# Four column groups for the left sums, one result partition, and two stores at the end of a column-sum kernel

## Chip, cores, metric

One core of one Trainium2 chip. The metric is device time in microseconds (us), the median of several executions. I also use the trace: the time from the landing of the last input byte to the end of the span, "the tail" below, is not disturbed by what the 620 us before it do. Landings, and the last increments of the stores (the steps by which a DMA counts up its semaphore as it completes), are read from the semaphore records of the trace; everything else from the profile.

## The reference

```python
def setup_inputs():
    batch, seq, dim = 32, 1024, 2048
    return {"grad_output": np.random.randn(batch, seq, dim).astype(np.float32)}

def reference(grad_output):
    return np.sum(grad_output, axis=(0, 1)).astype(np.float32)
```

32,768 rows of 2048 columns, 268 MB, are summed to one row.

## The kernel before

Rows stream in through one DMA queue into a ring in SBUF; VectorE adds them together. The last rows are instead summed over the 128 partitions by TensorE (a matmul with a column of ones), accumulating in PSUM. The very last rows come in a left part (1536 columns) and a right part (512), so that the left part can be finished while the right one still lands.

```python
LEFT = ((0, 512, 0), (512, 512, 1), (1024, 512, 2))      # first column, columns, column group
RIGHT = ((1536, 256, 2), (1792, 256, 3))
...
    for bank, pieces in enumerate((LEFT, RIGHT)):
        for lo, n, g in pieces:
            sums[lo] = psum[32 * g : 32 * g + 1, 512 * bank : 512 * bank + n]
...
    with nc.tensor.Fori(0, ROUNDS):
        for j, lane in enumerate(row_in):
            take(nc.tensor, lane)
            ... # one filler matmul of 256 columns into group 3
            matmuls(j * D, LEFT + RIGHT).then_inc(used, 1)
    matmuls(at * D, LEFT + RIGHT, wait=(step, n_step))
    for x, lo, pieces, lane, stop in final:
        then = (mm_left if pieces is LEFT else mm_right) if stop else None
        matmuls(x, pieces, lo, wait=(lane, 16), then=then)
...
    res = ring[:, res_at : res_at + 512]
    nc.scalar.copy(out=res[:96, :], in_=psum[:96, :512])._wait_ge(mm_left, len(LEFT)).then_inc(left, 1)
    half = res[96:97, :].rearrange("p (h n) -> p h n", h=2)
    nc.vector.tensor_copy(out=half[:, 0, :], in_=sums[RIGHT[0][0]])._wait_ge(mm_right, 1).then_inc(right_0, 1)
    nc.scalar.copy(out=half[:, 1, :], in_=sums[RIGHT[1][0]])._wait_ge(mm_right, 2).then_inc(right_1, 1)
    nc.sync.wait_ge(left, 1)
    nc.sync.wait_ge(right_0, 1)
    nc.sync.dma_start(out=out.rearrange("(g n) -> g n", g=4), in_=res[0:128:32, :])._wait_ge(right_1, 1).then_inc(done, 16)
```

The result lies in four rows, on partitions 0, 32, 64 and 96, and leaves in one store of four descriptors.

## Time and profile before

| | before |
|---|---|
| time, median of 3 | 629.28 us |
| span of the profiled run | 627.5 us |
| last input byte lands | 623.25 us |
| store's issue | 624.46 to 625.11 us |
| store's last increment | 626.22 us |
| tail (last input byte to end) | 4.30 us |

The span is filled by the input stream, at 428 GB/s. A line of the timeline reads: start, duration, engine, line, operation, output and input with shapes, count, and in brackets how long the engine sat idle and what ended it. SPq is the queue that issues the DMAs; the duration there is what the issue holds the queue, not the transfer.

### The profile page before, as it was taken

The numbers are of one execution on the slowest core, as the hardware profiler recorded it, in microseconds if no ns is written. First come the engines' busy times: TensorE is split into PE (matmuls) and PEld (weight loads), VectorE is DVE, ScalarE is ACT, GpSimd is POOL, SyncE is SP. The second block draws the span as 40 slices with busy tenths as digits, with TensorE's granted clock in tenths as the row PEclk, the third lists the DMA queues.
The fourth block names the chain that finished last, engine by engine and source line by source line (L and its number), as shares of the span: only waits on it lengthen the run. The fifth ranks groups of instructions, "written<-read, shape, count | busy, mean of one in ns | idle before, by whom it ended". The sixth has DMA issues, their size and how long they took to land. (4 is left out here: it accounts for less than half of the span.)

```text
span 627.5 us, 575 instructions
## 1 busy us (share of the span) xinstructions
PE 18.2 (3%) x136; PEld 4.9 (1%) x136; DVE 532.3 (85%) x68; ACT 2.4 (0%) x4; POOL 0.3 (0%) x5
## 2 busy tenths in 40 slices
PE   0000000000000000000000000000000000000055
PEld 0000000000000000000000000000000000000011
DVE  0349988889888898888988889988889888898994
ACT  0000000000000000000000000000000000000000
POOL 0000000000000000000000000000000000000000
PEclk9999999999999999999999999999999999999999
DMA  9999999999999999999999999999999999999996
GB/s 401 401 468 401 468 401 468 401 468 401 468 401 468 401 468 401 468 401 468 401 464 405 455 414 447 422 439 430 426 443 426 443 414 455 405 464 401 442 416 279
DMA packets 5912, 268.45 MB, mean 428 GB/s; under 512 B 660, under 2 KB 660, under 8 KB 1176
## 3 DMA queue, kind: packets, MB, share of 16 engines
q1 hardware_dynamic: 5912, 268.45, 99.1%
HBM read 268.44 MB, written 0.01 MB: 428 GB/s over the span
## 5 line engine op out<-in xcount | busy, mean ns | idle before, releaser
L118 DVE TENSOR_TENSOR ring<-ring 128x8192 f32<-128x8192 f32 (+2 forms) x65 | 528.6, 8134 | 84.9 <-DVEq L112 82.1
L183 PE MATMUL psum<-ring,ones 128*1 128x512 f32 (+1 forms) x120 | 18.2, 560 | 598.6 <-DMA ring<-in_grad_output_dram 598.5
L183 PEld LDWEIGHTS psum<-ring,ones 128*1 128x1 f32 x120 | 4.3, 86 | 608.4 <-DMA ring<-in_grad_output_dram 600.5
L200 PE MATMUL psum<-ring,ones 128*1 128x256 f32 x16 | 5.3, 412 | 7.0 <-PEq L112 7.0
L215 DVE COPY ring<-psum 1x256 f32<-1x256 f32 x1 | 0.4, 424 | 5.9 <-PE psum L183 5.9
L213 ACT COPY ring<-psum 96x512 f32<-96x512 f32 x1 | 0.6, 582 | 620.8 <-PE psum L183 620.8
L118 DVE TENSOR_TENSOR ring<-ring,head 128x2048 f32<-128x2048 f32 x1 | 2.3, 2292 | 0.1
L131 DVE MEMSET psum<- 128x1024 f32 x1 | 0.9, 912 | 1.2 <-SPq L121 1.2
L200 PEld LDWEIGHTS psum<-ring,ones 128*1 128x1 f32 x16 | 1.3, 92 | 10.0 <-issue 9.8
L211 ACT ACT_TABLE_LOAD x1 | 1.3, 1283 | 0.9 <-SPq L121 0.9
L216 ACT COPY ring<-psum 1x256 f32<-1x256 f32 x1 | 0.4, 365 | 0.3 <-PE psum L183 0.3
L211 ACT COPY warm<-ones 1x1 f32<-1x1 f32 x1 | 0.2, 190 | 0.0
L238 POOL MEMSET const-bfloat16-1.0<- 128x1 bf16 x1 | 0.1, 102 | 0.0
L238 POOL MEMSET const-uint8-127<- 128x1 uint8 x1 | 0.1, 102 | 0.0
L125 POOL MEMSET ones<- 128x1 f32 x1 | 0.1, 99 | 0.5 <-SPq L121 0.5
L238 POOL MEMSET const-float32-0.0<- 128x1 f32 x1 | 0.1, 99 | 0.2 <-issue 0.2
L238 POOL MEMSET const-float32-1.0<- 128x1 f32 x1 | 0.1, 99 | 0.0
## 6 DMA issues: line engine op xcount, KB each, us to landing
ring<-in_grad_output_dram SPq DMA_DIRECT2D x1, 5120.0 KB, 22.6
ring<-in_grad_output_dram SPq DMA_DIRECT2D x1, 4096.0 KB, 14.7
ring<-in_grad_output_dram SPq DMA_DIRECT2D x4, 1024.0 KB, 9.5
ring<-in_grad_output_dram SPq DMA_DIRECT2D x2, 768.0 KB, 13.5
head<-in_grad_output_dram SPq DMA_DIRECT2D x1, 1024.0 KB, 4.8
ring<-in_grad_output_dram SPq DMA_DIRECT2D x2, 256.0 KB, 14.5
ring<-in_grad_output_dram SPq DMA_DIRECT2D x30, 29.8
out_dram<-ring SPq DMA_DIRECT2D x1, 8.0 KB
```

The source lines that it names most:

```text
L118: return nc.vector.tensor_add(out=rows(at, n), in0=rows(at, n), in1=other)
L125: nc.gpsimd.memset(ones[:], 1.0).then_inc(one, 1)
L131: nc.vector.memset(psum[:, : 2 * 512], 0.0).then_inc(zero, 1)
L183: mat = nc.tensor.matmul(sums[lo], lhsT=ones[:], rhs=ring[:, x : x + n], start=start, stop=then is not None)
L200: nc.tensor.matmul(psum[96:97, 2 * 512 : 2 * 512 + FILLER], lhsT=ones[:], rhs=rows(j, 1)[:, :FILLER], start=True, stop=True)
L211: nc.scalar.copy(out=warm[:], in_=ones[0:1, :])._wait_ge(one, 1)
L213: nc.scalar.copy(out=res[:96, :], in_=psum[:96, :512])._wait_ge(mm_left, len(LEFT)).then_inc(left, 1)
L215: nc.vector.tensor_copy(out=half[:, 0, :], in_=sums[RIGHT[0][0]])._wait_ge(mm_right, 1).then_inc(right_0, 1)
L216: nc.scalar.copy(out=half[:, 1, :], in_=sums[RIGHT[1][0]])._wait_ge(mm_right, 2).then_inc(right_1, 1)
L238: nc = _bacc.Bacc("TRN2", target_bir_lowering=False, num_devices=1)
```

## The change

The intent: get the left sums out of the way early and in parallel, bring all sums to one partition, and let each part leave in a store of one descriptor.

```diff
-LEFT = ((0, 512, 0), (512, 512, 1), (1024, 512, 2))
+LEFT = ((0, 416, 0), (416, 416, 1), (832, 352, 2), (1184, 352, 3))
 RIGHT = ((1536, 256, 2), (1792, 256, 3))
 ...
-    res = ring[:, res_at : res_at + 512]
-    nc.scalar.copy(out=res[:96, :], in_=psum[:96, :512])._wait_ge(mm_left, len(LEFT)).then_inc(left, 1)
-    half = res[96:97, :].rearrange("p (h n) -> p h n", h=2)
-    nc.vector.tensor_copy(out=half[:, 0, :], in_=sums[RIGHT[0][0]])._wait_ge(mm_right, 1).then_inc(right_0, 1)
-    nc.scalar.copy(out=half[:, 1, :], in_=sums[RIGHT[1][0]])._wait_ge(mm_right, 2).then_inc(right_1, 1)
-    nc.sync.wait_ge(left, 1)
-    nc.sync.wait_ge(right_0, 1)
-    nc.sync.dma_start(out=out.rearrange("(g n) -> g n", g=4), in_=res[0:128:32, :])._wait_ge(right_1, 1).then_inc(done, 16)
+    res = ring[0:1, res_at : res_at + D]
+    def result(copy, lo, n, wait, then):
+        copy(out=res[:, lo : lo + n], in_=sums[lo])._wait_ge(*wait).then_inc(then, 1)
+    for copy, half in ((nc.scalar.copy, 0), (nc.vector.tensor_copy, 1)):
+        for i in range(2):
+            lo, n, _ = LEFT[2 * half + i]
+            result(copy, lo, n, (mm_left, len(LEFT)), left[half])
+        lo, n, _ = RIGHT[half]
+        result(copy, lo, n, (mm_right, half + 1), right[half])
+    nc.sync.wait_ge(left[0], 2)
+    nc.sync.dma_start(out=out[None, :cut], in_=res[:, :cut])._wait_ge(left[1], 2).then_inc(done, 16)
+    nc.sync.wait_ge(right[0], 1)
+    nc.sync.dma_start(out=out[None, cut:], in_=res[:, cut:])._wait_ge(right[1], 1).then_inc(done, 16)
 ...
-        nc.sync.wait_ge(done, 16)
+        nc.sync.wait_ge(done, 32)
```

(The declarations of the semaphores are cut.)

More of the change, by code (lines that the diff above doesn't have):

```diff
@@ L55 @@
     psum = psum_pool.tile([P, 3 * 512], fp32)
-    names = ("one", "zero", "vec", "step", "used", "mm_left", "mm_right", "left", "right_0", "right_1", "done")
-    one, zero, vec, step, used, mm_left, mm_right, left, right_0, right_1, done = (tc.alloc_semaphore(n) for n in names)
+    names = ("one", "zero", "vec", "step", "used", "mm_left", "mm_right", "done")
+    one, zero, vec, step, used, mm_left, mm_right, done = (tc.alloc_semaphore(n) for n in names)
     slot_in = [tc.alloc_semaphore(f"slot{s}") for s in range(SLOTS)]
@@ L65 @@
     last_in = [tc.alloc_semaphore(f"last{i}") for i in range(2 * LAST)]
+    left = [tc.alloc_semaphore(f"left{i}") for i in range(2)]
+    right = [tc.alloc_semaphore(f"right{i}") for i in range(2)]
     head_in = tc.alloc_semaphore("head")
```

## The prediction

> **What bounds the kernel now.** I read four views of the kernel before in this order: the page, the chain of waits, the timeline of the last 10 us, and the list of who the store queue waited for. I ask first what sets 627.5 us, and then what part of it the change can reach.
>
> The page:
>
> ```profile
> span 627.5 us, 575 instructions
> PE 18.2 (3%) x136; PEld 4.9 (1%) x136; DVE 532.3 (85%) x68; ACT 2.4 (0%) x4; POOL 0.3 (0%) x5
> DMA  9999999999999999999999999999999999999996
> q1 hardware_dynamic: 5912, 268.45, 99.1%
> ```
>
> The DMA row is nine tenths or more in 39 of 40 slices. The kernel streams 268 MB once; that stream is the bound, and the changed lines don't touch it. Only the last slice (6) is not full. So look at the end of the chain of waits (start us, us, what):
>
> ```profile
> 606.89 0.33 SPq L106
> 607.22 0.04 issue
> 607.26 0.43 SPq L106
> 607.70 0.04 issue
> 607.74 14.21 DMA ring<-in_grad_output_dram
> 621.95 0.04 issue
> 622.00 1.95 PE psum L183 x13
> 623.95 0.40 DVE ring L215
> ```
>
> The last loads are issued at about 607 to 609 and then sit behind the stream; the last but one half of the row lands at 621.95, and only after that does engine work set the end. Now the timeline of the end (start us, us, engine, line, operation, shapes, idle before):
>
> ```profile
> 622.00 0.10 PEld L183 LDWEIGHTS psum<-ring,ones 128*1 128x1 f32 x6 [1.01 <-DMA ring<-in_grad_output_dram]
> 623.14 0.58 ACT L213 COPY ring<-psum 96x512 f32<-96x512 f32 x1 [620.75 <-PE psum L183]
> 623.29 0.09 PEld L183 LDWEIGHTS psum<-ring,ones 128*1 128x1 f32 x4 [0.34 <-DMA ring<-in_grad_output_dram]
> 623.93 0.42 DVE L215 COPY ring<-psum 1x256 f32<-1x256 f32 x1 [5.93 <-PE psum L183]
> 623.97 0.36 ACT L216 COPY ring<-psum 1x256 f32<-1x256 f32 x1 [0.25 <-PE psum L183]
> 624.46 0.65 SPq L219 DMA_DIRECT2D out_dram<-ring  x1
> ```
>
> The left copy (623.14 to 623.72) is over before the right sums exist (623.89). What sets the end is: last right load at 623.25, two right matmul passes to 623.89, two short copies to 624.35, the store's issue 624.46 to 625.11, its landing, the program's end at 627.5. So 4.3 us of 627.5 lie after the last byte of input, 0.7%; all that the change can win or lose is a part of that. And the store queue's waits say what the store itself costs at the end:
>
> ```profile
> SPq L249 <- PEq L249: 0.7, 2, 0.5
> SPq L249 <- DMA out_dram<-ring: 0.2, 1, 0.2
> ```
>
> The final wait for the store is only 0.2 us long. The semaphore records of the trace show why: the store's issue ends at 625.11, the queue works through the section's closing semaphores until 626.06, and the store's last increment comes at 626.22. Most of its landing lies beside bookkeeping that comes after the issue anyway. Both move with the store's issue.
>
> **What the Trainium skill says.** "DMA: Bandwidth & Descriptors", section on why a DMA increments its semaphore by 16: a transfer uses as many engines as fit its slowest dimension, and the issuing sequencer itself writes the increments of the engines not used. The trace agrees for the store of four rows: its semaphore has five updates, one at 625.48 and four at 626.14, 626.14, 626.19 and 626.22; the loads of 128 rows have sixteen. A store of one descriptor should have two. The page gives no time for the extra write, but the issue of the store took 0.647 us against 0.327 to 0.432 us for the row loads of the end.
>
> "TensorE: Matmul & The Clock Gate", Part 3 on packing: matmuls in different column groups run side by side[...]. The trace agrees: three of 512 columns start at 618.306, 618.313 and 618.320, and the second passes of those three at 618.735, 0.43 us later.
>
> "Perfetto Trace Analysis", section Optimizing Scalar/DVE Operations: about half of the profiled latency of a copy's fixed part overlaps with the next instruction. No run here shows two copies back to back, so I use this for an estimate only.
>
> "PSUM — Partial Sum Buffer", Terms: two engines may not touch the same bank and quadrant at once. The change keeps to that: in bank 0 ScalarE reads groups 0 and 1, VectorE groups 2 and 3. The trace of before has no such pair, as its two right copies read different groups too.
>
> **The change part by part.**
>
> Left sums in four groups. Per row the busiest column group sets TensorE's time. Before: group 2 has 512 + 256 = 768 columns (the filler's 256 and right's 256 share group 3). The four row loads of before are issued at 603.02, 604.31, 605.60 and 606.89, each released by a finished row: 1.29 us per row, or 1.68 ns per column for the two passes. After: groups 2 and 3 have 352 + 256 = 608, and group 3 has 864 with the filler. So rows with filler cost 864 x 1.68 = 1.45 us (+0.16), rows without 608 x 1.68 = 1.02 us (-0.27). Does it matter? In the burst after 598.5 us, row loads may go out some 0.6 us later, but the first was issued at 603.02 and the DMA queue was full until 608.23, when the load before it landed; the last were issued 9 us and more before they were served. Hidden. In the paced part rows land 2.48 us apart, so 1.45 is hidden as well. At the end, from 618.3: 1.45 + 1.02 + 416 x 1.68 = 0.70, to about 621.6 with the last pass's tail, before the left load's landing at 621.95. Hidden. The final left matmuls: two passes of 416 columns instead of 512, 0.70 instead of 0.86, so the left sums are ready 0.16 us earlier: the copies can start at about 622.98 instead of 623.14. No gain in that by itself, as left wasn't last.
>
> All sums to one partition. ScalarE copies: 365 ns for 256 columns and 582 for 512 give 0.848 ns per column and 148 ns fixed, so 416 columns take 0.50 us; two, overlapping a little, end at about 622.98 + 0.93 = 623.91. VectorE: 424 ns for 256; its adds grow by 1.04 ns per column (2293 ns for 2048, 4425 for 4096), so 352 columns take 0.52 us; two from about 622.95 end at 623.93 to 624.00. The left work grows from one copy of 0.58 us to about 1.0 us on two engines, and ends about when the right sums come (623.89). Right copies: ScalarE starts at 623.97 as before, VectorE at 623.93 to 624.00 instead of 623.93: the right half is ready at 624.35 to 624.42, up to 0.07 later.
>
> Two stores of one descriptor. Left: both left waits are met at about 624.00, so its issue runs from 624.03; if it takes 0.647 us as the store now, to 624.68. Then the wait instruction and gaps (0.107 us before, from the last copy's end to the issue) and the right store starts at about 624.75 to 624.80 instead of 624.46: +0.3. The queue, not the data, then releases the right store. What follows shifts with it: packets, completion, end. One completion instead of the last of four gives back up to 0.09 us (626.14 against 626.22). Sum: +0.3 - 0.05 = about +0.2 us, within +0.15 to +0.35.
>
> **The rivals.** First, a store of one descriptor may be issued faster than one of four. For it: loads take 0.33 to 0.43. Against: those use all 16 engines, and one descriptor leaves 15 increments to write instead of 12. At 0.35 us per issue the left store is out of the way at 624.40, the right store starts with its data at 624.46 to 624.53, and a shorter issue brings its landing up to 0.3 us nearer: -0.25 us, 629.0. I give this 25%.
>
> Second, the single partition costs more than I reckon: two engines writing to one partition, or one DMA engine reading 6 KB. The left store has about 0.7 us of head start, so this would show only if left lands after right; +0.5 us, 629.8. 10%.
>
> Third, the filler in the now fuller group 3 delays the row loads after all. Against it: over 5 us of room in the queue. It would need the slow clock of the first rows (1.06 us for 512 columns there against 0.59 later) to last through the loop; even so it stays inside the room. Under 3%.
>
> Fourth, all cancels and the difference drowns in the spread of the three runs of before, 0.4 us. Compatible with any of these.
>
> **Range and chances.** The main case gives 629.28 + 0.2 = 629.5 us. The quick-issue rival sets the low side (629.0, less 0.15 for spread), the slow one the high side (629.8, and 0.25 for spread): 628.85 to 630.05. A change of 2% is 12.6 us, three times all the time after the last input byte. Nothing in the diff reaches the stream, so faster by 2% and slower by 2% get half a per cent each.
>
> **What would show it.** The changed kernel's timeline should show: ScalarE and VectorE with two left copies each from about 622.95 to 623.9 or 624.0, 0.5 us apiece; right copies at 623.93 to 624.00; two store issues in a row, the first at about 624.0, the second at about 624.75, both about 0.65 us long; the chain of waits ending in the queue's issue instead of a VectorE copy; row loads of the burst 1.45 us apart. Wrong would be: issues of 0.35 us (then the time falls), a second store released by a copy, a final wait for the store much longer than 0.2 us, or another landing time of the last load, measured from the span's start, which would mean that the stream itself moved and that my account of hidden work in the matmuls is false.

## The result

The changed kernel took 628.74 us, median of 6 (628.69 to 628.77); the kernel before took 629.31 in its 6 runs (629.18 to 629.69). The difference is 0.57 us. The ratio is 0.999 with a 95% interval of 0.9977 to 1.0003. (A ratio is the mean time of one kernel's fast runs over that of the other's in the same rounds, so not quite the ratio of the medians.) The interval is wider than the effect, but each of the six runs of the changed kernel was below the fastest run of before. The spans that the record lists are quieter than the times: 626.9 to 627.0 us in 15 of the 16 runs of the changed kernel (this timing, c1 and c2 below; the other has 627.5), 627.4 to 627.6 in all 27 runs of the kernel before that list one. The prediction said 629.5 with a range from 628.85: wrong in direction, and the time lies below the range.

The timeline of the end of the changed kernel:

```profile
621.91 0.10 PEld L185 LDWEIGHTS psum<-ring,ones 128*1 128x1 f32 x8 [1.13 <-DMA ring<-in_grad_output_dram]
...
622.93 1.41 ACT L216 COPY ring<-psum 1x416 f32<-1x416 f32 x3 [620.55 <-PE psum L185]
622.93 1.42 DVE L216 COPY ring<-psum 1x352 f32<-1x352 f32 x3 [5.02 <-PE psum L185]
623.20 0.09 PEld L185 LDWEIGHTS psum<-ring,ones 128*1 128x1 f32 x4 [0.53 <-DMA ring<-in_grad_output_dram]
624.04 0.32 SPq L226 DMA_DIRECT2D out_dram<-ring  x1
624.47 0.25 SPq L228 DMA_DIRECT2D out_dram<-ring  x1
```

Each engine's three copies are merged in one line: they follow each other with gaps of at most 0.03 us until 624.34 and 624.35, when the two copies of before ended too. The second store starts at 624.47, against 624.46 for the only store of before, but the issues take 0.32 and 0.25 us, not 0.65.

The chain of waits of the changed kernel (start us, us, what):

```profile
607.33 0.33 SPq L108
607.65 0.04 issue
607.70 0.43 SPq L108
608.13 0.04 issue
608.17 13.69 DMA ring<-in_grad_output_dram
621.87 0.04 issue
621.91 1.00 PE psum L185 x6
622.91 0.02 issue
622.93 0.52 DVE ring L216
623.45 0.03 issue
623.48 0.87 DVE ring L216 x2
```

It runs through the left matmuls and VectorE's three copies, not through the first store's issue. The queue is as late, though: the second store starts 0.105 us after the end of the first issue, in this trace and in c1, c2 and e8 below alike, and 0.12 us after its data; in e3, where no store goes ahead, the store starts 0.07 us after its data. So the first issue still costs the second store some 0.05 us (an estimate from these two). The row loads that the burst of matmuls releases go out later (607.33 for the last instead of 606.89), and it does not matter: the next load of the chain lands at 621.87 (621.95 before). The waits of the store queue have the same last line as before:

```profile
SPq L258 <- DMA out_dram<-ring: 0.2, 1, 0.2
```

Where the time came from, between the two traces, counted from the landing of the last input byte (623.25 before, 623.16 after):

| stretch | before | after | difference |
|---|---|---|---|
| landing to start of the last store's issue | 1.21 | 1.31 | +0.10 |
| that issue | 0.65 | 0.25 | -0.40 |
| end of issue to the store's last increment | 1.12 | 0.89 | -0.23 |
| from there to the end of the span | 1.32 | 1.31 | -0.01 |
| tail | 4.30 | 3.76 | -0.54 |

The input landed 0.09 us earlier in this trace. Over all 14 traces the landing lies between 623.13 and 623.32 us (leaving out one delayed share, told below), with the three of the changed kernel at 623.13 to 623.19; I don't count that as an effect.

### The profile page after: what moved, and what is told of

The parts are those of the page before. It is cut to its first block, busy times and chain, and to the rows that moved or that the text cites. A ratio compares the mean times of both kernels' runs of the same rounds, so it can differ in the third digit from the quotient of the medians.

```text
span 626.9 us, 628 instructions
## 1 busy us (share of the span) xinstructions
PE 18.8 (3%) x160; PEld 6.9 (1%) x160; DVE 533.2 (85%) x70; ACT 2.8 (0%) x5; POOL 0.3 (0%) x5
## 5 line engine op out<-in xcount | busy, mean ns | idle before, releaser
L185 PE MATMUL psum<-ring,ones 128*1 128x352 f32 (+2 forms) x144 | 18.8, 496 | 598.9 <-DMA ring<-in_grad_output_dram 598.9
L185 PEld LDWEIGHTS psum<-ring,ones 128*1 128x1 f32 x144 | 6.5, 86 | 607.6 <-DMA ring<-in_grad_output_dram 600.7
L216 DVE COPY ring<-psum 1x352 f32<-1x352 f32 (+1 forms) x3 | 1.4, 486 | 5.1 <-PE psum L185 5.0
L216 ACT COPY ring<-psum 1x416 f32<-1x416 f32 (+1 forms) x3 | 1.4, 453 | 620.6 <-PE psum L185 620.5
L202 PEld LDWEIGHTS psum<-ring,ones 128*1 128x1 f32 x16 | 1.2, 88 | 8.7 <-issue 8.0
```

Source lines behind the costliest of these rows:

```text
L185: mat = nc.tensor.matmul(sums[lo], lhsT=ones[:], rhs=ring[:, x : x + n], start=start, stop=then is not None)
L202: nc.tensor.matmul(psum[96:97, 2 * 512 : 2 * 512 + FILLER], lhsT=ones[:], rhs=rows(j, 1)[:, :FILLER], start=True, stop=True)
L216: copy(out=res[:, lo : lo + n], in_=sums[lo])._wait_ge(*wait).then_inc(then, 1)
```

## The experiments

The question is what makes an issue of 0.65 us into one of 0.25 to 0.32, and which parts of the change are needed for it. Theory A: the number of rows (descriptors, DMA engines) of the store. Theory B: several source partitions 32 apart. A further rival is that the gain comes from the split, or from the groups and copies. Theory D came from the results and was tested last. Twelve runs were made, of eleven kernels, five timed rounds each, four to a chip; "before" in the table is the kernel before on the same chip (nine runs).

| run | time | before | last store: source | issue | tail |
|---|---|---|---|---|---|
| e1 split alone | 629.05 | 629.22 | one row | 0.28 (left, three rows: 0.83) | 3.97 |
| e2 two and two rows | 629.45 | 629.22 | two rows 32 apart | 0.49 (first: 0.62) | 4.19 |
| e3 one store of 8 KB | 628.96 | 629.22 | one run | 0.32 | 3.94 |
| e4 written as four pieces | 629.03 | 629.22 | one run | 0.32 | 3.96 |
| c1 changed kernel | 628.76 | 629.25 | one row | 0.25 | 3.77 |
| e5 four pieces with gaps | 629.52 | 629.25 | one partition, gaps | 0.76 | 4.55 |
| e6 four neighbouring rows | 629.01 | 629.25 | partitions 0 to 3 | 0.35 | 3.96 |
| e7 left from GpSimd | 629.03 | 629.25 | one row | 0.32 | 4.07 |
| c2 changed kernel | 628.75 | 629.29 | one row | 0.25 | 3.74 |
| e8 three groups | 629.12 | 629.29 | one row | 0.25 | 4.03 |
| e9 right in four groups | 630.23 | 629.29 | one row | 0.25 | see below |
| e10 every second row | 629.45 | 629.29 | partitions 0, 2, 4, 6 | 0.73 | 4.38 |

Every interval includes 1; I read the tail first and use the medians as a check.

**The changed kernel again (c1, c2).** No edit.

> The changed kernel again, as the reference for the three others of this call. All theories: as in its first timing, 0.4 to 0.6 us under the kernel before, issues of 0.32 and 0.25 us.

> The changed kernel once more, as the reference for the others of this call: 0.4 to 0.6 us under the kernel before.

They came out 0.49 and 0.54 us below the kernel before, on chips 8 and 15. One of the ten runs (629.41) was late; the rest lie between 628.67 and 628.85. The 0.5 us is there, as the spans above show too, although one interval alone doesn't prove it.

**The split alone (e1).**

```diff
-    nc.sync.dma_start(out=rows4, in_=res[0:128:32, :])._wait_ge(right_1, 1).then_inc(done, 16)
+    nc.sync.dma_start(out=rows4[0:3, :], in_=res[0:96:32, :])._wait_ge(left, 1).then_inc(done, 16)
+    nc.sync.wait_ge(right_0, 1)
+    nc.sync.dma_start(out=rows4[3:4, :], in_=res[96:97, :])._wait_ge(right_1, 1).then_inc(done, 16)
```

> The kernel before, with the copies and groups as they were, but the left three rows leave in one store as soon as the left copy is done and the right row in a second store of one descriptor. Theory A (a store is issued the slower and lands the later the more rows, so DMA engines, it has, up to four; the first row is cheap): left issue about 0.54 us from 623.8, right issue 0.25 to 0.32 us from about 624.47, time 0.4 to 0.6 us under the kernel before, as the changed kernel. Theory B (what is slow is a source of several partitions 32 apart, what is quick is partition 0): right store also one partition, so quick, same time as the changed kernel; left issue 0.65. Theory C (the groups and the copies to one partition carry the gain): no gain beyond 0.15 us.

Its timeline:

```profile
623.10 0.58 ACT L213 COPY ring<-psum 96x512 f32<-96x512 f32 x1 [620.72 <-PE psum L183]
623.71 0.83 SPq L218 DMA_DIRECT2D out_dram<-ring  x1
623.90 0.42 DVE L215 COPY ring<-psum 1x256 f32<-1x256 f32 x1 [5.91 <-PE psum L183]
623.94 0.36 ACT L216 COPY ring<-psum 1x256 f32<-1x256 f32 x1 [0.26 <-PE psum L183]
624.67 0.28 SPq L220 DMA_DIRECT2D out_dram<-ring  x1
```

The right row's store is quick (0.28 us) even from partition 96. But the left store of three rows holds the queue for 0.83 us, to 624.54, though the right data are ready at 624.32: the right store starts at 624.67. This is what I had predicted for the changed kernel, in another one. The split alone wins 0.17 us in the medians, 0.33 in the tail. Three rows slower than four was expected by neither theory.

**Two and two rows (e2).** As e1, with rows 0 and 1 in the first store and rows 2 and 3 in the second.

> The kernel before with two stores of two rows each. Theory A: the issue of each store lies between that of one row (0.25 to 0.32) and that of four (0.65), about 0.40 to 0.43 us, and the time between the two kernels, about 0.3 us under the kernel before. Theory B (several partitions 32 apart are slow as such): issue about 0.65 us each; the second starts late and the time is 0 to 0.3 us over the kernel before. Theory of size (a store of 4 KB instead of 8 is quicker): about 0.3 to 0.4 us under, with an issue of 0.65.

The issues took 0.62 and 0.49 us. The tail is 0.11 us under that of before, but the timed runs scatter from 629.08 to 630.19, so the time says little (the spans, 627.3 to 627.5 us, lie just under those of before, 627.4 to 627.6). The order 0.32 (one row), 0.62 (two), 0.83 (three), 0.65 (four), for a queue that had been idle, is not the steady growth of theory A.

**One store of 8 KB, as one run and as four pieces (e3, e4).** The changed kernel with one store of everything; in e4 the access is written as four pieces of 2 KB.

```diff
-    nc.sync.dma_start(out=out[None, :cut], in_=res[:, :cut])._wait_ge(left[1], 2).then_inc(done, 16)
+    nc.sync.wait_ge(left[1], 2)
     nc.sync.wait_ge(right[0], 1)
-    nc.sync.dma_start(out=out[None, cut:], in_=res[:, cut:])._wait_ge(right[1], 1).then_inc(done, 16)
+    nc.sync.dma_start(out=out[None, :], in_=res)._wait_ge(right[1], 1).then_inc(done, 16)   # e4: both sides cut in 4
```

> The changed kernel with one store of one descriptor of 8 KB instead of two stores. Theory A: one issue of 0.25 to 0.32 us from about 624.47; the one packet takes four times 84 ns, some 0.25 us more than the right store of the changed kernel: time 0.2 to 0.35 us over the changed kernel, still 0.2 to 0.35 under the kernel before. Theory C' (the gain is the split, so that only 2 KB leave at the end): no better than the kernel before.

> As the one store of 8 KB from one partition, but written as four pieces of 2 KB. If the four pieces reach the queue as four: theory A gives an issue of 0.65 us and the time of the kernel before (within 0.15 us); theory B (the partitions are what costs) an issue of about 0.3 us. If the pieces are merged again into one descriptor, the same as one store of 8 KB.

The store of e3:

```profile
624.53 0.32 SPq L228 DMA_DIRECT2D out_dram<-ring  x1
```

Its one packet took 0.31 us, against 0.08 for the 2 KB of the changed kernel's right store, and the increment came 1.39 us after the start of the issue, against 1.14. So one descriptor without the split wins about half: 0.26 us in the medians, 0.35 in the tail. It is not the size either: 8 KB are issued in 0.32 us here, 4 KB took 0.62 and 0.49 in e2. In e4 the pieces had been merged to one descriptor of 8192 bytes, so it decided nothing between A and B; it repeats e3 (3.96 against 3.94).

**Four pieces with gaps on one partition (e5), four neighbouring partitions (e6), every second partition (e10).** All three give a wrong result; only the store's source is changed, in e5 from e4, in e6 and e10 from the kernel before.

```diff
+    gaps = ring[0:1, res_at : res_at + 4 * 528].rearrange("p (h n) -> p h n", h=4)[:, :, :512]   # e5
-    in_=res[0:128:32, :]
+    in_=res[0:4, :]      # e6
+    in_=res[0:8:2, :]    # e10
```

> Wrong result on purpose: one store from one partition, but read as four pieces of 2 KB with a gap between them, so that they can't be merged into one descriptor. Theory A (the number of pieces, so of DMA engines, makes the issue slow): issue about 0.65 us, five updates of the store's semaphore, time as the kernel before, within 0.15 us (its start is about the same). Theory B (several source partitions make it slow): issue about 0.32 us and a time 0.3 to 0.6 us under the kernel before.

> Wrong result on purpose: the kernel before with its store reading partitions 0 to 3 instead of 0, 32, 64 and 96. Theory A (four rows, whatever their distance): issue 0.65 us and the time of the kernel before within 0.1 us. Theory B in the form that the distance of 32 partitions makes it slow: issue 0.33 to 0.45 us and 0.3 to 0.5 us under the kernel before.

> Wrong result on purpose: the kernel before with its store reading partitions 0, 2, 4 and 6. Theory D (a source whose pieces don't adjoin is issued slowly, whatever the step): issue about 0.65 us, time as the kernel before within 0.1 us. Theory of the step of 32 (the pieces must lie in different groups of 32 partitions to be slow): issue 0.35 us and 0.2 to 0.3 us under the kernel before, as with four neighbouring partitions.

The stores of e5, e6 and e10, one line of each timeline:

```profile
624.44 0.76 SPq L229 DMA_DIRECT2D out_dram<-ring  x1
```

```profile
624.38 0.35 SPq L219 DMA_DIRECT2D out_dram<-ring  x1
```

```profile
624.51 0.73 SPq L219 DMA_DIRECT2D out_dram<-ring  x1
```

All three move four pieces of 2 KB, and the store's semaphore has five updates in each. Four neighbouring partitions are issued in 0.35 us, so it is not the number of rows: theory A falls. One partition with gaps takes 0.76 us, so it is not the number of partitions: theory B falls in its general form. A step of two takes 0.73, so it is not the step of 32. What is left, and what all stores fit, is theory D: a source whose pieces don't adjoin (a step over partitions, or gaps in one) costs 0.49 to 0.83 us to issue, one that is a single run or neighbouring partitions 0.25 to 0.35. Why it is so no run shows. The single change of e6, neighbours instead of a step, is worth 0.24 us in the medians and 0.33 in the tail; the expectation had 0.3 to 0.5. The times of e5 and e10 were 0.27 and 0.16 us over the kernel before, more than the 0.15 and 0.1 expected, with issues about 0.1 us longer. And e5 has the groups and the copies of the changed kernel: with a slow store they gain nothing, its tail is 0.26 us longer than that of before.

The landing has a price of its own. From the end of the issue to the last increment, one row of 2 KB took 0.89 to 0.91 us (e1, c1), one run of 8 KB 1.07 (e3), two rows 1.12 (e2), four rows 1.08 (e6) and 1.12 (before), four pieces with gaps 1.24 (e5). So a larger last store landed later; whether by its bytes or its pieces, no run separates. The start of the first packet follows theory D as well: on the store queue it came 0.59 to 0.63 us after the end of the issue where the pieces don't adjoin, 0.42 to 0.48 where they do (but 0.58 for the right store of e7, below).

**The left store from GpSimd (e7).** As e1, with the left store on GpSimd's queue and a semaphore of its own.

> The split alone, with the left three rows issued by GpSimd instead of the store queue, so that only the right row's store is on that queue. If the queue was what held back the right store in the split alone (started 0.2 us after its data), the right store now starts at about 624.45 with an issue of 0.32 us, and as nothing delays the right copies the time is equal to the changed kernel or 0.1 us under it, provided that the left store lands before the right one. If GpSimd's store takes over 2 us from 623.7, the final wait is for it and the time is over that of the kernel before.

```profile
623.95 0.63 POOL L218 DMA_DIRECT2D out_dram<-ring  x1 [622.90 <-ACT ring L213]
624.39 0.32 SPq L220 DMA_DIRECT2D out_dram<-ring  x1
```

The right store now starts with its data: 1.19 us after the last landing, against 1.45 in e1 and 1.31 in the changed kernel. So the queue was what held it in e1. GpSimd starts the left store 0.29 us after the left copy's end, and that store is complete at 625.72. What is late is the right one: its last increment comes 1.18 us after the end of its issue, at 625.90, where the right stores of e1 and c1 took 0.89 to 0.91. The store queue's waits show it:

```profile
SPq L251 <- DMA out_dram<-ring: 0.5, 1, 0.5
```

The packets of both stores lie in the same 0.3 us of the trace here; that they hinder each other is likely, not shown. The tail is 4.07 us, longer than e1's 3.97. Moving the store to another queue gave nothing over e1; the expectation of equal or better than the changed kernel was wrong, and so was its reason for a failure, a late left store.

**Three left groups (e8).** The changed kernel with the left groups of before; ScalarE copies two of 512 columns, VectorE one.

> The changed kernel with the left sums in three groups of 512 as before: ScalarE copies two of them, VectorE one. If the four groups are needed to get the left copies out of the way of the right ones: left sums ready 0.16 us later, ScalarE's two copies of 0.58 us end at about 624.2, its right copy starts there instead of at 624.0, so the right store starts 0.2 to 0.3 us later and the time is 0.2 to 0.3 us over the changed kernel. If only the stores matter: as the changed kernel within 0.1 us.

```profile
623.04 1.56 ACT L216 COPY ring<-psum 1x512 f32<-1x512 f32 x3 [620.66 <-PE psum L185]
...
624.31 0.32 SPq L228 DMA_DIRECT2D out_dram<-ring  x1
624.74 0.25 SPq L230 DMA_DIRECT2D out_dram<-ring  x1
```

ScalarE's three copies now end at 624.60 instead of 624.30 in c2, and both stores start 0.31 us later than in c2 (624.31 and 624.74 against 624.00 and 624.43). Time 0.37 us over c2, tail 0.28. Of the 0.31 us, 0.03 is a later landing, 0.12 is later left sums (passes of 512 columns instead of 416), and 0.16 is ScalarE's two left copies, 1.17 us instead of 1.02. So the four groups bring the left sums earlier and split the copies to one partition evenly, and keep those copies from costing what the quick store wins. Three groups with an even split of the copies were not tried.

**The right part in four groups (e9).** A try at something better: 640 right columns in four groups of 160, 1408 left ones.

> The changed kernel with 640 right columns in four groups of 160 instead of 512 in two of 256, and 1408 left ones. If the right copies of the changed kernel are held back by 0.09 us by the left ones, and the right matmuls are paid by their width: two passes of 160 instead of 256 save 0.16 us, the left copies are over before the right sums, two right copies per engine cost 0.1 us more than one: time about 0.1 us under the changed kernel. If neither: the same, or up to 0.1 us over it for the two more copies.

```profile
622.74 0.96 ACT L216 COPY ring<-psum 1x384 f32<-1x384 f32 x2 [620.35 <-PE psum L185]
...
624.72 0.10 PEld L185 LDWEIGHTS psum<-ring,ones 128*1 128x1 f32 x8 [2.02 <-DMA ring<-in_grad_output_dram]
...
625.19 0.59 ACT L216 COPY ring<-psum 1x160 f32<-1x160 f32 x2 [1.50 <-PE psum L185]
625.28 0.67 DVE L216 COPY ring<-psum 1x160 f32<-1x160 f32 x2 [1.53 <-PE psum L185]
625.98 0.25 SPq L229 DMA_DIRECT2D out_dram<-ring  x1
```

The last right load landed only at 624.68. Fifteen of its sixteen shares were there by 623.32; the last was 1.37 us later. In that stretch, from 622 us, the DMA view of this run has one transfer that isn't the kernel's:

```profile
q8 instruction: 1, 0.02, 2.1%
```

It is a fetch of 16 KB of instructions; its packet ran from 622.51 to 623.60, 1.09 us, and the increment packet of the late share (4 bytes, by which a DMA engine counts up the semaphore) started at 623.58. The traces of the changed kernel (three), e3, e4 and e5 have such a fetch too (from 622.40 to 622.55, 1.08 to 1.10 us), and there no share was late. That the fetch shared a DMA engine with the late share, and so held it back, I infer from the times; the records read here don't show the engine, and no run tested it. It also explains only a part: the late increment packet started 0.74 us after the one before it (622.85), and its increment came 1.10 us after that start, where those of the load's other shares took 0.45 to 0.51 (paired in order of time). For the rest the record has no cause. Four of the five runs of e9 were above 630 us. The fifth, at 628.99, is 0.24 over the median of c2, and the tail after the late share is 3.76, that of the changed kernel: no gain even without the delay. The changed kernel is the best that I ran.

## Why the prediction was wrong

Its steps, one by one.

The bound, and what lies outside the change's reach: right. Nothing moved before the tail beyond the scatter of landings.

The matmuls: right. The row loads of the burst are 1.455 us apart (1.45 predicted), the left sums were copied from 622.93 (622.98), and all was hidden.

The copies: right within 0.05 us. ScalarE's left copies took 0.50 us each and VectorE's 0.52, but one after the other, without the overlap of the estimate: two took 1.02 us on ScalarE instead of 0.93. That the clock times fit all the same is luck, as the copies started 0.05 us earlier than predicted. The right copies started at 623.97 and 623.94. Since the last load had landed 0.09 us earlier, the right half was ready 0.09 us later after it than in the kernel before, a little more than the 0.07 that the prediction allowed.

The stores: this is the step that failed. The prediction put it as "its issue runs from 624.03; if it takes 0.647 us as the store now, to 624.68", and built the main case on it. The first store did start at 624.04, but its issue took 0.322 us and the second's 0.249. So the queue was free at 624.37, just when the right data were ready (624.35), and the second store started at 624.47, 0.12 us after its data, as the store of before (0.11), not at 624.75 to 624.80. The +0.3 of the sum was +0.01 on the clock, and the shorter issue took 0.40 off. (The sum as written, +0.3 - 0.05, is 0.25, not 0.2; that is not what failed.) I had read the 0.65 us as the price of a store, with the extra increments as its likely reason. But one descriptor leaves the queue more increments to write by the prediction's own count, 15 instead of 12, and is quick. The 0.65 belonged to this source, four rows 32 partitions apart: the same store from neighbouring partitions took 0.35 (e6), from one run 0.32 (e3), and with any gap 0.73 to 0.76 (e5, e10).

The first rival had the right mechanism, at 25%, and was itself too small: 629.0 against 628.74. Two sizes were short: it took 0.35 us for an issue, and the last store's was 0.25; and the prediction gave back only "up to 0.09 us" for one completion instead of four, where the time from the end of the issue to the last increment fell by 0.23 us. How the total splits is shown by e3 and c1: a single descriptor for everything wins about 0.26 us, the split of that into an early large and a late small store another 0.23 to 0.28 by the medians (c1 and c2 win 0.49 and 0.54 in all, on other chips) and 0.18 by the tails (3.94 against 3.76). The other rivals did not appear: the left store landed 0.24 us before the right one, and the fuller group 3 delayed no load that counted.

The range failed too. Its low side was the rival's time less 0.15 us for spread; the spread of the six runs was only 0.08 us, but the rival's own error was 0.26.

## What to carry to other kernels

When a duration from the profile is carried over to a changed instruction, ask what it is the price of: an issue time read off one transfer is that of its shape, and here the shape was what the change altered. A last store should leave from one run of one partition, or from neighbouring partitions, and be small, with the bulk sent ahead of it as soon as it is ready; but the ahead-sent store must itself be quick to issue, or it holds back the last one on the same queue (e1). Extra copies that make this possible are free only while they end before the last sums are ready (e8).

## What the Trainium skill lacked or had wrong

- "DMA: Bandwidth & Descriptors" (section on why a DMA increments its semaphore by 16): that the sequencer writes the increments of the engines not used agrees with the traces, two updates for one descriptor and five for four rows. The page gives no issue time by the shape of the source. Measured on the store queue: 0.25 to 0.35 us for a single run or four neighbouring partitions, 0.49 to 0.83 us for rows or pieces with a gap between them, and not steadily growing with their number (two 0.62, three 0.83, four 0.65).
- The same page, on the landing of small stores: from the end of the issue to the last increment 0.89 us for one descriptor of 2 KB, 1.07 for one of 8 KB, 1.08 to 1.24 for four of 2 KB. The page gives a fixed cost of about 2 us for the GpSimd path and a first-byte latency of about 0.6 us for the sync queue's (here 0.72 to 1.43 us from the start of an issue to its first packet), not this time.
- "Perfetto Trace Analysis", Optimizing Scalar/DVE Operations: about half of a copy's fixed time should overlap with the next. In the changed kernel VectorE's third copy started 0.07 us before the end of the second, but its second started 0.03 us after the end of the first. ScalarE's three followed each other with gaps of 0.02 to 0.03 us.
- "Runtime: NRT & Kernel Launch", Instruction fetch mechanics: it says that a sequencer fetches its instructions by a DMA queue of its own, in blocks of 16 KiB, and the traces agree (one packet of 16,384 bytes near the end of the input in the changed kernel, e3, e4, e5 and e9). It gives no time for a fetch, here 1.08 to 1.10 us. That the fetch delayed a load in e9, by up to 0.74 of the 1.37 us, is inferred.
